# A weighted sum of two expert outputs: three buffers of 16 tokens for four of 12, a small first tile in a block of its own, and a double last-but-one store

## The chip, the cores and the metric

The kernel runs on one core of a Trainium2 chip. The core has a vector engine (VectorE, in the profile DVE), a scalar engine (ScalarE, ACT), and SyncE (SP), which here only issues DMAs. Transfers between the large memory (HBM) and the on-chip memory (SBUF, 128 partitions) are carried out by 16 DMA engines; SP and ACT each have a queue of their own that feeds all 16. The metric is the device time of one execution in microseconds; less is better.

## The reference

```python
"expert_outputs": np.random.randn(batch, seq, k, hidden)   # 16 x 1024 x 2 x 512, float32
"combine_weights": np.random.randn(batch, seq, k)          # 16 x 1024 x 2

weights = combine_weights[..., np.newaxis]
return np.sum(expert_outputs * weights, axis=2).astype(np.float32)
```

There are 16 x 1024 = 16,384 tokens. Each has two rows of 512 values (4 KB together), each row is multiplied by its own weight, and the two are added to one output row of 2 KB. 67.1 MB of rows are read and 33.6 MB are written.

## The kernel before

The tokens are spread over the 128 partitions, 128 tokens on each. In HBM they form two blocks: in the first, 120 neighbouring tokens belong to each partition (so the partitions' rows lie 120 x 4 KB = 480 KB apart in the input and 240 KB apart in the output); in the second, the last 8 per partition (32 KB and 16 KB apart). The function `rows` makes both views, and picks the block by the token's number.

Work goes in ten tiles of `J = 12` tokens per partition and a last one of `LAST = 8`. Each tile `et` is one of four buffers of 48 KB per partition (`bufs=4`). For each tile:

- SP loads it (line 75). One partition's part is contiguous in HBM, so it is one packet of 48 KB. The first tile is loaded in two pieces of 2 and 10 tokens, and the first of these is cut into packets of 4 KB by `max_dma_last_dim`.
- Tiles 0 to 8: VectorE multiplies all rows by their weights (line 84) and adds the two halves (line 85). Tile 9: ScalarE scales the first rows (line 92), VectorE the second ones (line 107) and adds (line 108). Tile 10, the last: ScalarE scales a token's first row (line 92), and VectorE does the second row's product and the sum in one instruction (line 96).
- The result `ot` overwrites the lower half of the tile's own buffer, and is stored from there: by ACT's queue in tiles 0 to 8 (line 86), by SP's in the last two (line 109).

A load into a buffer waits until the store of the tile that had it four tiles earlier has landed. The order on each engine is set by the framework's scheduler, which also inserts all waits. Before the first tile, ACT's queue writes 16 rows of zeros into the output (`ahead`, line 58; the results overwrite them later) and then loads the weights in two pieces, 120 and 8 KB (line 62).

Of the kernel before, what the change touches and what calls it, by code (L numbers as in the profile page):

```python
# [1 line left out]

# [4 lines left out]


@with_exitstack
def kernel(  # L10
    ctx: ExitStack,
    tc: tile.TileContext,
    expert_outputs: bass.AP,
    combine_weights: bass.AP,
    out: bass.AP,
):

    nc = tc.nc  # L20
    b, s, k, h = expert_outputs.shape
    assert k == 2
    n = b * s
    P = nc.NUM_PARTITIONS
    per = n // P
    assert per * P == n
    J, LAST = 12, 8
    main = per - LAST
    assert main % J == 0
    eo = expert_outputs.rearrange("b s k h -> (b s) (k h)")  # L30
    cw = combine_weights.rearrange("b s k -> (b s) k")
    o = out.rearrange("b s h -> (b s) h")

    def rows(x):

        a = x[0 : P * main, :].rearrange("(p t) f -> p t f", p=P)
        b = x[P * main : n, :].rearrange("(p t) f -> p t f", p=P)
        return lambda t, c: a[:, t : t + c, :] if t < main else b[:, t - main : t - main + c, :]

    eo, cw, o = rows(eo), rows(cw), rows(o)  # L40

    dt = mybir.dt.float32
    mult = mybir.AluOpType.mult
    add = mybir.AluOpType.add
    copy = mybir.ActivationFunctionType.Copy

    last = main // J

    wpool = ctx.enter_context(tc.tile_pool(name="w", bufs=1))
    ipool = ctx.enter_context(tc.tile_pool(name="in", bufs=4))  # L50

    wt = wpool.tile([P, per * k], dt)


    zt = wpool.tile([16, 128], dt)
    nc.vector.memset(zt, 0.0)  # L56
    first = out.rearrange("b s h -> (b s) h")[0 : P * main, :].rearrange("(q t) h -> q (t h)", q=16)
    ahead = nc.scalar.dma_start(out=first[:, 0:128], in_=zt)  # L58

    with tc.issue_after(ahead.ins):  # L60
        for t, c in ((0, main), (main, LAST)):
            nc.scalar.dma_start(
                out=wt[:, k * t : k * (t + c)].rearrange("p (t k) -> p t k", k=k), in_=cw(t, c)
            )
        warm = wpool.tile([P, 1], dt)
        nc.scalar.activation(out=warm, in_=nc.const_aps.tensor(1.0, (P, 1), dt), func=copy)  # L66

    for g in range(last + 1):
        et = ipool.tile([P, J, k * h], dt)

        ot = et.rearrange("p j f -> p (j f)")[:, 0 : J * h].rearrange("p (j f) -> p j f", f=h)
        t0, c = g * J, J if g < last else LAST

        for a, m in ((0, 2), (2, c - 2)) if g == 0 else ((0, c),):
            nc.sync.dma_start(  # L75
                out=et[:, a : a + m],
                in_=eo(t0 + a, m),
                max_dma_last_dim=k * h * 4 if g + a == 0 else None,
            )
        if g < last - 1:  # L80

            wb = wt[:, g * J * k : (g + 1) * J * k].unsqueeze(2).to_broadcast([P, J * k, h])
            ek = et.rearrange("p j (k h) -> p (j k) h", k=k)
            nc.vector.tensor_tensor(out=ek, in0=ek, in1=wb, op=mult)  # L84
            nc.vector.tensor_tensor(out=ot, in0=et[:, :, 0:h], in1=et[:, :, h : 2 * h], op=add)  # L85
            nc.scalar.dma_start(out=o(t0, c), in_=ot)
            continue


        for i in range(c):  # L90
            t = t0 + i
            nc.scalar.activation(  # L92
                out=et[:, i, 0:h], in_=et[:, i, 0:h], func=copy, scale=wt[:, 2 * t : 2 * t + 1]
            )
            if g == last:
                nc.vector.scalar_tensor_tensor(  # L96
                    out=ot[:, i, :],
                    in0=et[:, i, h : 2 * h],
                    scalar=wt[:, 2 * t + 1 : 2 * t + 2],
                    in1=et[:, i, 0:h],  # L100
                    op0=mult,
                    op1=add,
                )
        if g < last:
            w1 = wt.rearrange("p (t k) -> p t k", k=k)[:, t0 : t0 + c, 1:2]
            x1 = et[:, :, h : 2 * h]
            nc.vector.tensor_tensor(out=x1, in0=x1, in1=w1.to_broadcast([P, c, h]), op=mult)  # L107
            nc.vector.tensor_tensor(out=ot, in0=et[:, :, 0:h], in1=x1, op=add)  # L108
        nc.sync.dma_start(out=o(t0, c), in_=ot[:, 0:c])


# [1 line left out]
_INS = ['expert_outputs', 'combine_weights']  # L113
_OUTS = [((16, 1024, 512), 'float32')]


# [23 lines left out]
```

## Time and profile before

| | |
|---|---|
| Median of 3 runs | 239.11 us (239.08 to 239.12) |
| Span of the profiled execution, first to last instruction | 237.3 us |
| What lies around the span, against the median | 1.8 us |
| DVE busy | 194.1 us (82%) |
| ACT busy | 14.0 us (6%) |
| HBM read, written | 67.24 MB, 33.56 MB |
| DMAs of `et` loads | 2, then 10 tokens; nine of 12 tokens (6144 KB); one of 8 |
| Median time from issue to landing, loads of 12 tokens | 29.9 us |
| Median time from issue to landing, stores on ACT's queue | 33.0 us |

The profile is of one execution. Its span leaves out a little time at both ends, so times are compared through the medians of the runs, and places through the span. Queue q1 is SP's and q10 is ACT's. The share of a DMA queue is the time that its packets took, as a part of what 16 engines have in the span; a packet is one contiguous row that one engine moves, or the four bytes with which an engine signals its end. The granted TensorE clock is 1.000 and plays no part, as there are no matmuls. Times from issue to landing overlap each other: a DMA that was queued early waits long.

### The profile page before, as it was taken

What the parts mean: (1) busy time and instruction counts of PE and PEld (TensorE: products, weight loads), DVE (VectorE), ACT (ScalarE), POOL (GpSimd) and SP (SyncE); (2) the same over time, 40 slices, a digit from 0 to 9 for tenths busy, and PEclk for the clock granted to TensorE, in tenths of its full rate; (3) what the DMA queues carried; (4) which work ended last, traced back from release to release, by engine and by line L of the source; (5) the groups of instructions that cost most, each with busy time, mean ns of one, the idle gap of its engine ahead of it and who ended that gap; (6) DMA issues with size and microseconds to landing.
All of it is one profiled execution on the core that took longest, in us unless ns stands there. A gap on an engine that the chain in (4) does not pass through costs nothing.

```text
span 237.3 us, 157 instructions
## 1 busy us (share of the span) xinstructions
DVE 194.1 (82%) x29; ACT 14.0 (6%) x22; POOL 0.2 (0%) x4
## 2 busy tenths in 40 slices
DVE  0008999999999999999999889969996998785710
ACT  2000000000000000000000000000000000740800
POOL 0000000000000000000000000000000000000000
DMA  7999999989899999999898999999998979999997
GB/s 289 452 474 398 398 448 480 398 356 505 352 443 435 427 464 464 398 398 530 348 514 348 447 418 443 464 464 398 398 522 348 522 344 451 464 398 442 406 434 309
DMA packets 3760, 100.80 MB, mean 425 GB/s; under 512 B 544, under 2 KB 688, under 8 KB 944
## 3 DMA queue, kind: packets, MB, share of 16 engines
q1 hardware_dynamic: 2144, 72.35, 71.0%
q10 hardware_dynamic: 1616, 28.45, 27.9%
HBM read 67.24 MB, written 33.56 MB: 425 GB/s over the span
## 4 chain that ended last, share of the span: by engine, by line
DMA 59%; DVE 34%; ACT 2%; ACTq 0%; DVEq 0%; issue 0%; SPq 0%
DMA out_dram<-et 29%; DMA et<-in_expert_outputs_dram 23%; DVE et L84 22%; DVE et L85 11%; DMA wt<-in_combine_weights_dram 7%; ACT et L92 2%; DVE et L96 1%; DVEq L135 0%; ACTq L135 0%; ACTq L58 0%; DVE zt L56 0%; DVEq L84 0%; SPq L75 0%; ACTq L92 0%
## 5 line engine op out<-in xcount | busy, mean ns | idle before, releaser
L84 DVE TENSOR_TENSOR et<-et,wt 128x12288 f32<-128x12288 f32 x9 | 116.6, 12955 | 24.1 <-DMA wt<-in_combine_weights_dram 17.5
L85 DVE TENSOR_TENSOR et<-et 128x6144 f32<-128x6144 f32 x9 | 59.0, 6557 | 0.3
L92 ACT ACTIVATE et<-et,wt 128x512 f32<-128x512 f32 x20 | 12.5, 708 | 208.6 <-DMA et<-in_expert_outputs_dram 208.6
L96 DVE SCALAR_TENSOR_TENSOR et<-et,wt 128x512 f32<-128x512 f32 x8 | 5.6, 746 | 3.9 <-ACT et L92 3.6
L107 DVE TENSOR_TENSOR et<-et,wt 128x6144 f32<-128x6144 f32 x1 | 6.6, 6557 | 2.3 <-DMA et<-in_expert_outputs_dram 2.3
L108 DVE TENSOR_TENSOR et<-et 128x6144 f32<-128x6144 f32 x1 | 6.6, 6558 | 0.9 <-ACT et L92 0.9
L66 ACT ACT_TABLE_LOAD x1 | 1.3, 1283 | 2.4 <-issue 2.4
L56 DVE MEMSET zt<- 16x128 f32 x1 | 0.2, 165 | 0.8 <-PEq L124 0.8
L66 ACT ACTIVATE warm<-const-float32-1.0 128x1 f32<-128x1 f32 x1 | 0.2, 202 | 0.0
L124 POOL MEMSET const-bfloat16-1.0<- 128x1 bf16 x1 | 0.1, 102 | 0.0
L124 POOL MEMSET const-uint8-127<- 128x1 uint8 x1 | 0.1, 101 | 0.0
L124 POOL MEMSET const-float32-0.0<- 128x1 f32 x1 | 0.1, 99 | 0.2 <-issue 0.2
L124 POOL MEMSET const-float32-1.0<- 128x1 f32 x1 | 0.1, 98 | 0.0
## 6 DMA issues: line engine op xcount, KB each, us to landing
et<-in_expert_outputs_dram SPq DMA_DIRECT2D x9, 6144.0 KB, 29.9
out_dram<-et ACTq DMA_DIRECT2D x9, 3072.0 KB, 33.0
et<-in_expert_outputs_dram SPq DMA_DIRECT2D x1, 5120.0 KB, 17.0
et<-in_expert_outputs_dram SPq DMA_DIRECT2D x1, 4096.0 KB, 25.1
out_dram<-et SPq DMA_DIRECT2D x1, 3072.0 KB, 14.6
out_dram<-et SPq DMA_DIRECT2D x1, 2048.0 KB, 10.0
et<-in_expert_outputs_dram SPq DMA_DIRECT2D x1, 1024.0 KB, 5.0
wt<-in_combine_weights_dram ACTq DMA_DIRECT2D x1, 120.0 KB, 17.0
```

The costliest lines, as they stand in the source:

```text
L56: nc.vector.memset(zt, 0.0)
L66: nc.scalar.activation(out=warm, in_=nc.const_aps.tensor(1.0, (P, 1), dt), func=copy)
L84: nc.vector.tensor_tensor(out=ek, in0=ek, in1=wb, op=mult)
L85: nc.vector.tensor_tensor(out=ot, in0=et[:, :, 0:h], in1=et[:, :, h : 2 * h], op=add)
L92: nc.scalar.activation(out=et[:, i, 0:h], in_=et[:, i, 0:h], func=copy, scale=wt[:, 2 * t : 2 * t + 1])
L96: nc.vector.scalar_tensor_tensor(out=ot[:, i, :], in0=et[:, i, h : 2 * h], scalar=wt[:, 2 * t + 1 : 2 * t + 2], in1=et[:, i, 0:h], op0=mul ...
L107: nc.vector.tensor_tensor(out=x1, in0=x1, in1=w1.to_broadcast([P, c, h]), op=mult)
L108: nc.vector.tensor_tensor(out=ot, in0=et[:, :, 0:h], in1=x1, op=add)
L124: nc = _bacc.Bacc("TRN2", target_bir_lowering=False, num_devices=1)
```

## The change

- The tile sizes become 4, 12 and seven times 16 tokens. The first tile of 4 is a block of its own in HBM (its partitions' rows lie 16 KB apart in the input), and the other 124 tokens per partition are a second block (496 KB apart in the input, 248 KB in the output).
- One allocation `et` holds three rooms of 16 tokens each; tile g uses room g modulo 3. The load of tile g + 3 follows the store of tile g.
- Every tile is computed as the last one was: ScalarE scales the first row of a token, VectorE does the second product and the sum. Line by line these are the operations of lines 92 and 96 before.
- The seventh tile (number 6) is computed from its last token down, and its result lies in the upper half of its room; the eighth tile's result lies in the lower half of the next room. The two adjoin, and one DMA stores both, 32 tokens or 64 KB per partition.
- The last two stores go through SP's queue, the others through ACT's. The weights of the first tile (4 KB) are loaded by ACT's queue, the rest (124 KB) by SP's, right behind the load of the first tile. The first load isn't cut into packets of 4 KB any more.
- `tc.manual_schedule()` makes every engine issue in the order written. The waits are still inserted by the framework.

```diff
-    J, LAST = 12, 8
-    main = per - LAST
+    ROOM, ROOMS = 16, 3
+    TILES = [4, 12, 16, 16, 16, 16, 16, 16, 16]
+    STORES = [[0], [1], [2], [3], [4], [5], [6, 7], [8]]
+    main = TILES[0]
+    starts = [sum(TILES[:g]) for g in range(len(TILES))]
...
-    wpool = ctx.enter_context(tc.tile_pool(name="w", bufs=1))
-    ipool = ctx.enter_context(tc.tile_pool(name="in", bufs=4))
+    pool = ctx.enter_context(tc.tile_pool(name="all", bufs=1))
+    et = pool.tile([P, ROOMS * ROOM, k * h], dt)
+    halves = et.rearrange("p j (k h) -> p (j k) h", k=k)
...
+    def load(g):
+        at, c = g % ROOMS * ROOM, TILES[g]
+        nc.sync.dma_start(out=et[:, at : at + c], in_=eo(starts[g], c))
+
+    def weights(q, t, c):
+        q.dma_start(out=wt[:, k * t : k * (t + c)].rearrange("p (t k) -> p t k", k=k), in_=cw(t, c))
+
+    def combine(g, up):
+        at, c = g % ROOMS * ROOM, TILES[g]
+        base = k * at + (ROOM if up else 0)
+        for i in range(c - 1, -1, -1) if up else range(c):
+            t = k * (starts[g] + i)
+            x0, x1 = halves[:, k * (at + i), :], halves[:, k * (at + i) + 1, :]
+            nc.scalar.activation(out=x0, in_=x0, func=copy, scale=wt[:, t : t + 1])
+            nc.vector.scalar_tensor_tensor(
+                out=halves[:, base + i, :], in0=x1, scalar=wt[:, t + 1 : t + 2], in1=x0, op0=mult, op1=add
+            )
+        return base
...
+    with tc.manual_schedule():
+        nc.vector.memset(zt, 0.0)
+        ahead = flat[0 : P * main, :].rearrange("(q t) h -> q (t h)", q=16)
+        nc.scalar.dma_start(out=ahead[:, 0:128], in_=zt)
+        weights(nc.scalar, 0, main)
+        nc.scalar.activation(out=warm, in_=nc.const_aps.tensor(1.0, (P, 1), dt), func=copy)
+        load(0)
+        weights(nc.sync, main, per - main)
+        for g in range(1, ROOMS):
+            load(g)
+        for j, st in enumerate(STORES):
+            bases = [combine(g, up=len(st) == 2 and g == st[0]) for g in st]
+            c = sum(TILES[g] for g in st)
+            q = nc.sync if j >= len(STORES) - 2 else nc.scalar
+            q.dma_start(out=o(starts[st[0]], c), in_=halves[:, bases[0] : bases[0] + c, :])
+            for g in st:
+                if g + ROOMS < len(TILES):
+                    load(g + ROOMS)
```

The old loop over tiles, with its loads, its three ways to compute and its stores (lines 68 to 109), is removed.

More of the change, by code (lines that the diff above doesn't have):

```diff
@@ L26 @@
     assert per * P == n
-    J, LAST = 12, 8
-    main = per - LAST
[L29 to L32, printed above, removed]
-    def rows(x):
[L36 to L40, printed above, removed]
+    ROOM, ROOMS = 16, 3
+    TILES = [4, 12, 16, 16, 16, 16, 16, 16, 16]
+    STORES = [[0], [1], [2], [3], [4], [5], [6, 7], [8]]
+    assert sum(TILES) == per and [g for st in STORES for g in st] == list(range(len(TILES)))
+    main = TILES[0]
+    starts = [sum(TILES[:g]) for g in range(len(TILES))]
+    def rows(x):
+        first = x[0 : P * main, :].rearrange("(p t) f -> p t f", p=P)
+        second = x[P * main : n, :].rearrange("(p t) f -> p t f", p=P)
+        return lambda t, c: first[:, t : t + c, :] if t < main else second[:, t - main : t - main + c, :]
+    flat = out.rearrange("b s h -> (b s) h")
+    eo = rows(expert_outputs.rearrange("b s k h -> (b s) (k h)"))
+    cw = rows(combine_weights.rearrange("b s k -> (b s) k"))
+    o = rows(flat)
     dt = mybir.dt.float32
@@ L45 @@
     copy = mybir.ActivationFunctionType.Copy
-    last = main // J
-    wpool = ctx.enter_context(tc.tile_pool(name="w", bufs=1))
-    ipool = ctx.enter_context(tc.tile_pool(name="in", bufs=4))
[L52 to L63, printed above, removed]
-            )
-        warm = wpool.tile([P, 1], dt)
-        nc.scalar.activation(out=warm, in_=nc.const_aps.tensor(1.0, (P, 1), dt), func=copy)
@@ L68 @@
[L68 to L109, printed above, removed]
@@ new lines @@
+    pool = ctx.enter_context(tc.tile_pool(name="all", bufs=1))
+    et = pool.tile([P, ROOMS * ROOM, k * h], dt)
+    halves = et.rearrange("p j (k h) -> p (j k) h", k=k)
+    wt = pool.tile([P, per * k], dt)
+    zt = pool.tile([16, 128], dt)
+    warm = pool.tile([P, 1], dt)
+    def load(g):
[3 more added lines that the diff above has]
+        q.dma_start(out=wt[:, k * t : k * (t + c)].rearrange("p (t k) -> p t k", k=k), in_=cw(t, c))
@@ new lines @@
+    with tc.manual_schedule():
[3 more added lines that the diff above has]
+        weights(nc.scalar, 0, main)
+        nc.scalar.activation(out=warm, in_=nc.const_aps.tensor(1.0, (P, 1), dt), func=copy)
+        load(0)
[5 more added lines that the diff above has]
+            c = sum(TILES[g] for g in st)
+            assert bases[-1] == bases[0] + sum(TILES[g] for g in st[:-1])
+            q = nc.sync if j >= len(STORES) - 2 else nc.scalar
[3 more added lines that the diff above has]
+                    load(g + ROOMS)
```

## The prediction

> **What bounds the kernel now.** I read the page first, its summary of engines, its 40 slices and its DMA section.
>
> ```profile
> DVE 194.1 (82%) x29; ACT 14.0 (6%) x22; POOL 0.2 (0%) x4
> ...
> DMA  7999999989899999999898999999998979999997
> ...
> DMA packets 3760, 100.80 MB, mean 425 GB/s; under 512 B 544, under 2 KB 688, under 8 KB 944
> ## 3 DMA queue, kind: packets, MB, share of 16 engines
> q1 hardware_dynamic: 2144, 72.35, 71.0%
> q10 hardware_dynamic: 1616, 28.45, 27.9%
> ```
>
> VectorE is busy 82% of the span, but the two queues together hold the 16 DMA engines for 71.0 + 27.9 = 98.9% of it. The traffic sets the time, not the arithmetic. The next question is where the missing 1.1% lies, so I cut the span into windows (columns: microseconds, busy time of each engine, granted clock, DMA share, GB/s).
>
> ```profile
> 0.00:1.75 1.75, 0.17 (x1) 0.00 (x0) 0.20 (x4) 1.00 0.00 0
> 1.75:2.75 1.00, 0.00 (x0) 0.37 (x1) 0.00 (x0) 1.00 0.90 143
> ...
> 38.00:41.00 3.00, 3.00 (x2) 0.00 (x0) 0.00 (x0) 1.00 0.84 344
> 41.00:48.00 7.00, 7.00 (x1) 0.00 (x0) 0.00 (x0) 1.00 1.02 414
> 48.00:200.00 152.00, 145.11 (x16) 0.00 (x0) 0.00 (x0) 1.00 1.01 435
> ...
> 236.20:237.30 1.10, 0.00 (x0) 0.00 (x0) 0.00 (x0) 1.00 0.00 0
> ```
>
> Nothing moves in the first 1.75 us and the last 1.1 us; between them the engines never stand still, and from 48 to 200 us they hold 435 GB/s. (A large packet counts where it starts, so short windows jump.) Last, who waits, and how the last tile's arithmetic runs, from the waits of the SP queue and the timeline:
>
> ```profile
> SPq L75 <- DMA out_dram<-et: 174.1, 7, 45.8
> ```
>
> ```profile
> 38.04 141.23 ACTq L86 DMA_DIRECT2D out_dram<-et  x8
> ...
> 219.90 5.01 ACT L92 ACTIVATE et<-et,wt 128x512 f32<-128x512 f32 x8 [9.48 <-DMA et<-in_expert_outputs_dram]
> 220.66 5.78 DVE L96 SCALAR_TENSOR_TENSOR et<-et,wt 128x512 f32<-128x512 f32 x8 [3.65 <-ACT et L92]
> ```
>
> The loads wait for stores to free their buffers, yet the load queue always holds an earlier load meanwhile. ScalarE and VectorE overlap: eight tokens take 226.44 - 219.90 = 6.54 us together.
>
> **The packet account.** The trace's packet records give the price of size. One packet is one contiguous row of one partition: 16 KB 611 ns, 24 KB 912, 32 KB 1213, 40 KB 1514, 48 KB 1815. Each further 8 KB costs 301 ns, that is 27.2 GB/s per engine. The records of one engine overlap by 3 to 4 ns, so a packet costs some 4.6 ns beyond its bytes; a semaphore packet of 4 bytes (one per engine and DMA, 9 ns) shifts the next by some 6 ns. Per engine before:
> - bytes: 100.80 MB / 16 / 27.2 GB/s = 231.63 us
> - 3760 packets less 26 DMAs x 16 semaphores = 3344, 209 per engine, x 4.6 ns = 0.96
> - 26 semaphores x 6.2 ns = 0.16
> - start: the 16 packets of 4 KB take 194 ns in the mean where 159 is usual, 0.57; the engines' first packets start 0.14 after the first one in the mean
> - 44 load packets around the first store (40.9 to 47 us) take up to 2.33 us instead of 1.82: 0.61 per engine
>
> Sum 234.07. With the first packet at 1.79, the mean engine ends at 235.9, which the records show (235.7 to 236.14). The rest of the span of 237.3 follows the last packet: landing, semaphores, the closing drain. The median of 239.11 lies 1.8 us over the span, and I keep that.
>
> **The change, part by part.**
> - Bytes: the same. The first zero write and the weights (120 + 8 KB become 4 + 124 KB) sum to the same bytes.
> - Packets: a load of 4, 12 or 16 tokens is 128 rows of 16, 48 or 64 KB; nine loads give 1152. Eight stores give 1024, weights 256, zero write 16: 2448, or 153 per engine. 56 fewer x 4.6 ns = -0.26 us. By the line above, a 64 KB packet takes 2.417 us and the store of 32 tokens is 64 KB too.
> - DMAs: 9 + 8 + 2 + 1 = 20 instead of 26; six semaphores x 6.2 ns = -0.04. The Trainium skill (DMA: Bandwidth & Descriptors, Anatomy of one DMA) puts a fixed cost of about 2.0 us on each DMA of the GpSimd path; charged end to end, six fewer would bring 12 us. No row here shows such a charge between queued DMAs: the next packet begins 3 ns after a semaphore's.
> - The start: eight packets of 16 KB replace sixteen of 4 KB on each engine. Only the first one or two of an engine were slow (195 to 1071 ns, then 159). Bounds: the 0.57 us vanishes, or comes again when the second tile first touches the block with the wide pitch. I take it as unchanged, for the slow packets come first whatever their row.
> - The first store: bounds 0 and twice 0.61 (store of tile 0, then of tile 1, in another block). I take it unchanged, by the row of before's own second block: the 32 KB load packets took 1213 ns and its 16 KB store packets 611, without any excess.
> - Pitch: before, partitions lie 480 KB apart (stores 240), after it 496 (248). At 480, only those 44 of 1152 load packets were far off 1815 ns, by 0.61 x 16 / 44 = 0.22 us or 12%. Bounds: nothing, and 12% on all loads of the wide block (124 tokens, 149 us), 18 us. I take nothing, the row of the other 1108.
> - The Trainium skill (same page, Latency and other measured facts) warns of row pitches at large powers of two and gives 207 GB/s at 512 KB against 214 padded. If 496 KB behaved so, 3.4% of the wide block's 224 us of traffic, 7.6 us, would be added (an estimate from that page). No run here shows 512 KB.
> - Arithmetic: VectorE's two passes (19.5 us per 12 tokens) and their 194 us give way to 128 scalings at 708 ns on ACT and 128 fused steps at 0.72 us pace on DVE, some 91 and 92 us. It all lies beside DMA. The weights no longer land after 17 us, and that too is worth nothing: in those 17 us the engines were moving loads.
> - Rooms: three of 16 tokens instead of four of 12, the same 192 KB per partition. This can only cost, by leaving the load ring empty. A tile takes 0.78 + 16 x 0.72 = 12.3 us. Load g+3 can be issued once store g lands: some 12.3 + 8 x (2.42 + 1.21) = 29.0, plus 1.5 for issue and landing, 43 us after load g landed. Meanwhile the ring holds loads g+1 and g+2, 2 x 19.35 us, and store g itself takes 9.7 us of the engines: 48.4 of work for 43 us. The cover is 5.5 us at least. At the start: store 0 is issued near 11 us, its first packet follows some 5.3 us later (43.3 after 38.04 before), eight packets beside 48 KB ones need 17: landed near 34, while loads 0 to 2 keep the ring busy beyond 43.
> - The end, on SP: behind the wait for store 5, SP holds load 8, behind it the two last stores. The double store comes 12.3 + 1.5 us after load 7 landed; load 8 runs 19.35 us meanwhile, cover 5.5. The last store comes as long after load 8; the double store runs 19.34 us, cover 5.5. Each us beyond a cover costs one us.
> - ACT's queue: a store waits for DVE's last step, behind it stand the scalings of the next tile. Some 1 us per tile, within those covers. The small weights on SP stand behind load 0: eight packets of 45 ns, already counted in the bytes.
>
> Sum: -0.26 - 0.04 = -0.30; span 237.0, time 239.11 - 0.30 = **238.8 us**. A measurement of this kernel tells 0.2%, 0.48 us, from no change, so this counts as the same.
>
> **Rivals.**
> - The cold spots shrink (faster, 0.28). Contiguous first rows and a small first store may remove most of 0.57 + 0.61: 238.8 - 1.2 = 237.6 at best, 238.2 with half. For it: the excess lies exactly at the first load and the first store. Against: it may belong to being first, not to the rows. It counts as faster from a further 0.18 us on.
> - Cold spots come twice (slower, 0.08): the wide block pays anew in loads and stores, +1.2, 240.0. Against: before's second block paid nothing.
> - ACT and DVE take turns instead of overlapping (slower, 0.07). Place: the last three tiles. One token then takes 0.708 + 0.746 = 1.45 us, a tile 23.3: 11 us later than reckoned, which exceeds the three covers of 5.5 by 5.5 each, 16.5 us: 255. It decides from a pace of 0.72 + 5.5/16 = 1.06 us per token. Against: the timeline shows 5.78 us for eight.
> - The pitch slows packets (slower, 0.05): +18, 257 at the worst; it decides from (0.30 + 0.48) / 149 = 0.5% on each load packet. Against: 1108 packets at a like pitch.
> - 64 KB rows are cut in two, so the change does not do what it says (0.05): 64 more packets per engine x 4.6 ns = +0.29, 239.1, the same.
> - The forecast keeps 0.47.
>
> Same 0.52, faster 0.28, slower 0.20. The range reaches down to half of the cold spots gone, 238.2 less 0.1 for a bit more, and up to 239.7, some three quarters of the cold spots paid anew; the dear slow cases stay outside.
>
> **What would show it.** After: 2448 + 20 x 16 = 2768 packets, 1728 on q1 and 1040 on q10; 3792 if 64 KB is cut. DMA share 0.00 only in the first 1.8 and last 1.2 us; DVE and ACT busy near 90 us each; load packets of 64 KB at 2.417 us. A DMA window below 0.9 around the loads of the eighth and ninth tile, or near the end, means a cover was too short. Load packets above 2.42 us all along mean the pitch. A span off by over 0.5 us with full windows would mean that the start or the first stores changed.

## The result, and the profile after

The changed kernel takes 240.57 us in the median of seven runs (240.47 to 241.04), the kernel before 239.12 beside it: a ratio of 1.0061, interval 1.0047 to 1.0074. It is slower by 1.45 us, where 0.3 us less was forecast. The profiled execution took 240.50 us with a span of 238.7, 1.36 us more than before's 237.3.

The page of after, the same parts as shown of before:

```profile
span 238.7 us, 415 instructions
...
DVE 87.3 (37%) x129; ACT 80.9 (34%) x130; POOL 0.2 (0%) x4
...
DMA  7997999899999999989899999989898989898994
...
DMA packets 2771, 100.83 MB, mean 422 GB/s; under 512 B 448, under 2 KB 592, under 8 KB 592
## 3 DMA queue, kind: packets, MB, share of 16 engines
q1 hardware_dynamic: 1728, 79.82, 77.9%
q10 hardware_dynamic: 1040, 20.98, 20.4%
q14 instruction: 3, 0.02, 0.0%
```

The packets are as counted, 2768 on two queues. But there is a third queue, q14, of kind instruction, with three packets that before's page did not have. I take them for the program's own code, fetched while it runs (below, a fetch): their number follows the number of instructions in the runs below. The instructions went from 157 to 415. In the windows (microseconds, busy time of each engine, clock, DMA share, GB/s) the engines still never stand still together, and hold the same rate:

```profile
0.00:1.75 1.75, 0.17 (x1) 0.00 (x0) 0.20 (x4) 1.00 0.06 19
...
60.00:200.00 140.00, 55.10 (x82) 49.55 (x80) 0.00 (x0) 1.00 1.00 435
200.00:237.00 37.00, 11.69 (x18) 9.91 (x16) 0.00 (x0) 1.00 0.94 408
237.00:238.70 1.70, 0.00 (x0) 0.00 (x0) 0.00 (x0) 1.00 0.00 0
```

The forecast covers held. From the timeline:

```profile
1.62 180.50 SPq L62 DMA_DIRECT2D et<-in_expert_outputs_dram  x8
...
189.00 9.91 ACT L73 ACTIVATE et<-et,wt 128x512 f32<-128x512 f32 x16 [15.34 <-DMA et<-in_expert_outputs_dram]
189.75 11.07 DVE L74 SCALAR_TENSOR_TENSOR et<-et,wt 128x512 f32<-128x512 f32 x16 [14.17 <-ACT et L73]
200.85 19.70 SPq L96 DMA_DIRECT2D out_dram<-et  x2
208.35 9.91 ACT L73 ACTIVATE et<-et,wt 128x512 f32<-128x512 f32 x16 [9.44 <-DMA et<-in_expert_outputs_dram]
```

ACT and VectorE overlap: 16 tokens take 200.82 - 189.00 = 11.8 us (12.3 reckoned). The double store was issued at 200.85, while load 8 ran until 208.3: 7.5 us of cover.

**Where the time went** shows only when the sixteen DMA engines are taken apart. The records don't name the engine, but each packet begins 3 or 4 ns before the one ahead of it on the same engine ends, so they can be chained engine by engine. The excess of a packet is its time less the usual time of its size; a gap is time between two data packets of a chain. This account, in us, is worked out from the records of the two profiled executions:

| | before, mean of 16 engines | after, mean | after, slowest engine |
|---|---|---|---|
| excess in the first 10 us | 0.57 | 0.99 | 0.96 |
| excess from 10 to 33 us | 0.02 | 0.07 | 0.00 |
| excess from 33 to 50 us (first large store) | 0.58 | 0.54 | 0.38 |
| excess later | 0.01 | 0.13 | 0.99 |
| gaps in the chain | 0.06 | 0.06 | 0.60 |
| last packet ends at | 235.94 | 236.15 | 237.29 |

Before's slowest engine ended at 236.14, 0.21 behind the mean; after's ended 1.14 behind it. So the 1.36 us of span are: the mean engine +0.21, the slowest engine's lag +0.93, and the time from the last packet to the span's end +0.21 (1.20 before, 1.41 after; I have not traced that last part). The slowest engine of after is the one that carried two of the three instruction packets: each of 8 KB and 309 ns leaves a gap of 302 ns, and the 64 KB packet behind it takes 530 or 457 ns longer than 2418. That is 0.60 + 0.99 = 1.59 us; in its other rows that engine was 0.26 better than the mean, and the mean itself has 0.19 in these two, so 1.14 is left. The windows show the late engine too, first before, then after:

```profile
235.00:236.00 1.00, 0.00 (x0) 0.00 (x0) 0.00 (x0) 1.00 0.62 262
236.00:237.00 1.00, 0.00 (x0) 0.00 (x0) 0.00 (x0) 1.00 0.00 0
```

```profile
235.00:236.00 1.00, 0.00 (x0) 0.00 (x0) 0.00 (x0) 1.00 0.38 164
236.00:237.00 1.00, 0.00 (x0) 0.00 (x0) 0.00 (x0) 1.00 0.08 33
```

### The profile page after: what moved, and what is told of

It reads as the page before. It is cut to its first block, busy times and chain, and to the rows that moved or that the text cites. A ratio compares the mean times of both kernels' runs of the same rounds, so it can differ in the third digit from the quotient of the medians.

```text
span 238.7 us, 415 instructions
## 1 busy us (share of the span) xinstructions
DVE 87.3 (37%) x129; ACT 80.9 (34%) x130; POOL 0.2 (0%) x4
## 3 DMA queue, kind: packets, MB, share of 16 engines
q1 hardware_dynamic: 1728, 79.82, 77.9%
q10 hardware_dynamic: 1040, 20.98, 20.4%
## 4 chain that ended last, share of the span: by engine, by line
DMA 80%; DVE 7%; ACT 4%; issue 1%; ACTq 0%; DVEq 0%; SPq 0%
DMA et<-in_expert_outputs_dram 39%; DMA out_dram<-et 38%; DVE et L74 7%; ACT et L73 4%; DMA wt<-in_combine_weights_dram 3%; DVEq L125 0%; ACTq L125 0%; ACTq L83 0%; DVE zt L80 0%; SPq L62 0%; DVEq L74 0%; ACTq L73 0%
## 5 line engine op out<-in xcount | busy, mean ns | idle before, releaser
L74 DVE SCALAR_TENSOR_TENSOR et<-et,wt 128x512 f32<-128x512 f32 x128 | 87.2, 745 | 132.0 <-ACT et L73 130.2
L73 ACT ACTIVATE et<-et,wt 128x512 f32<-128x512 f32 x128 | 79.4, 707 | 135.4 <-DMA et<-in_expert_outputs_dram 130.0
```

The lines of the kernel that those rows point to most:

```text
L73: nc.scalar.activation(out=x0, in_=x0, func=copy, scale=wt[:, t : t + 1])
L74: nc.vector.scalar_tensor_tensor(out=halves[:, base + i, :], in0=x1, scalar=wt[:, t + 1 : t + 2], in1=x0, op0=mult, op1=add)
```

## The experiments

Times are medians, ratios are against the kernel before on the same chip. A lag, below, is how far the slowest engine is behind the middle one when both signal the end of a load or store on q1 (0.19 us in before from 50 us on, 1.34 at the end of after).

**Which part is it: first block, first packets, double store?** Three runs on after, each one edit.

after_4k:
```diff
-        nc.sync.dma_start(out=et[:, at : at + c], in_=eo(starts[g], c))
+        ... max_dma_last_dim=k * h * 4 if g == 0 else None
```


> After, with the first load cut into rows of 4 KB as before; all else unchanged. If the excess at the start (0.985 us per engine against 0.565 before) comes from the 16 KB packets, it falls back to some 0.57 and the time by 0.4 to 240.2. If it comes from the first tile's narrow block, it stays, and the time stays at 240.6.

Measured 240.78 us, ratio 1.0069 (1.0051 to 1.0087). The excess in the first 10 us stayed at 0.90. The packet size of the first load is not what makes the start slower.

after_wide:
```diff
-    main = TILES[0]
+    main = per - TILES[-1]                       # the weights then come in three pieces
```


> After, with the blocks moved: the first 112 tokens of a partition are one block (448 KB apart), so the first tile of 4 is read with the wide pitch, and the last tile of 16 is a block of its own; the weights come in three pieces. If the narrow first block makes the start slower, the excess at the start falls to some 0.57 us and the time by 0.4 to 240.2. If the packet size does, the time stays at 240.6; if the wide pitch of 496 KB costs something later, it falls too, but with the start unchanged.

Measured 240.66 us, ratio 1.0059 (1.0042 to 1.0077). The excess at the start fell to 0.69, most of the way to the 0.57 expected of the first block, but the excess from 33 to 50 us rose from 0.54 to 1.06. What was won was lost 30 us later, and the time stayed.

after_single:
```diff
-    STORES = [[0], [1], [2], [3], [4], [5], [6, 7], [8]]
+    STORES = [[0], [1], [2], [3], [4], [5], [6], [7], [8]]
```


> After with the seventh and eighth tile stored one by one (on SP's queue) instead of as one row of 64 KB; instructions nearly the same. Theory of the instruction fetches: 240.6, as after, the same three fetches. Rival (the double store or its packets make the end late): faster by 0.5 or more, 240.1 or below.

Measured 240.59 us, ratio 1.0062 (1.0050 to 1.0074), as after. The double store shows no price and no gain here.

**The first block in before.** before_narrow:
```diff
-        a = x[0 : P * main, :]
+        a = x[0 : P * J, :]        # and so for the second block and the weights
```


> The kernel before with its blocks moved: the first tile of 12 tokens is a block of its own (48 KB apart), the other 116 tokens are the second block (464 KB apart); instructions and tiles unchanged. If the narrow first block costs 0.3 to 0.4 us at the start, as in after against after_wide (0.985 against 0.685 us of excess), the excess there rises from 0.57 to some 0.9 and the time to 239.5. If that excess is made up later (around 35 to 45 us, where after_wide lost what it had won), or comes from the small first tile, the time stays at 239.1.

Measured 240.06 us (239.53 to 240.76), ratio 1.0039 (1.0024 to 1.0055). Slower, but not at the start: the excess there was 0.48, so a narrow first block of 12 tokens costs nothing there. It was 0.89 instead of 0.58 from 33 to 50 us, and seven of the engines took the first store packet one place earlier in their order than the rest. Neither of the two expectations had this.

**Instruction fetches in before.** The two clean ones add ACT instructions that nobody waits for (the order on ACT and VectorE is fixed as written here):
```diff
             nc.scalar.dma_start(out=o(t0, c), in_=ot)
+            for _ in range(40 if g < 8 else 0):      # 12 in the other
+                nc.scalar.activation(out=warm, in_=nc.const_aps.tensor(1.0, (P, 1), dt), func=copy)
```


> The kernel before with 40 one-element ACT instructions behind each of the first eight stores (320 more; some 9 us per tile in which ACT would idle), VectorE and all DMAs unchanged. ACT then holds some 370 instructions. Theory of the instruction fetches: three fetches of 8 KB on q14, all for ACT and on one DMA engine, which falls behind the other fifteen by 3 x 0.25 to 0.55 us; the time rises by 0.7 to 1.6 us to 239.8 to 240.7. Rival (instruction count plays no part): 239.1.

> The same with 12 instead of 40 (96 more, ACT some 150 as in after): one fetch. Theory of the instruction fetches: one engine falls behind by 0.25 to 0.55 us, and as the slowest engine of before is 0.19 us behind the middle one already, the time rises by 0.1 to 0.5, to 239.2 to 239.6. Rival: 239.1.

With 40: 240.81 us, ratio 1.0068 (1.0055 to 1.0081). With 12: 239.34 us, ratio 1.0013 (1.0005 to 1.0022). The pages show that nothing else changed; first the one with 40, then the one with 12:

```profile
q1 hardware_dynamic: 2144, 72.35, 70.6%
q10 hardware_dynamic: 1616, 28.45, 27.7%
q14 instruction: 3, 0.02, 0.0%
```

```profile
q1 hardware_dynamic: 2144, 72.35, 71.0%
q10 hardware_dynamic: 1616, 28.45, 27.9%
q14 instruction: 1, 0.01, 0.0%
```

Everything but q14 is before's, to the packet. In the one with 40 the middle engine ends at 236.03 us, against 235.95 in before; one engine's lag climbs from 0.27 to 0.47, 1.11 and 1.76 us behind the three fetches (61.7, 122.1 and 185.4 us). The time follows that one engine: +1.67 us for a lag of +1.57. The windows show it as a single engine's share after the rest have ended (1/16 is 0.06; a packet counts where it starts):

```profile
235.00:236.00 1.00, 0.00 (x0) 0.00 (x0) 0.00 (x0) 1.00 0.69 295
236.00:237.00 1.00, 0.00 (x0) 0.00 (x0) 0.00 (x0) 1.00 0.04 16
237.00:238.00 1.00, 0.00 (x0) 0.00 (x0) 0.00 (x0) 1.00 0.04 16
```

Two more runs on before were to show the same, and a second effect came on top. before_many:
```diff
+    def tiny(acts, dves):   # one-element instructions
             nc.scalar.dma_start(out=o(t0, c), in_=ot)
+            tiny(12, 18)
```


> The kernel before with 108 one-element ACT instructions and 162 one-element VectorE fills added behind the tiles, so that its engines hold about as many instructions as after; DMAs, tiles and rows unchanged. Theory of the instruction fetches: three more 8 KB packets of kind instruction appear on q14 in mid run, each holds up one DMA engine by 0.3 to 0.5 us, and the time rises by 0.4 to 1.2 us (239.5 to 240.3). Rival (the packets of 64 KB, the first block or the double store are the cause, the instruction count plays no part): 239.1, the same as before.

before_tok (all tiles computed as the last one):
```diff
-        if g < last - 1:        # the two large VectorE instructions, and those of tile 9
...
+        (nc.scalar if g < last - 1 else nc.sync).dma_start(out=o(t0, c), in_=ot[:, 0:c])
```


> The kernel before with only the arithmetic of the change: all tiles are computed token by token (ACT scales the first row, VectorE does product and sum), so that ACT and VectorE hold some 150 and 200 instructions; blocks, tiles of 12, four buffers, packets and stores as before. Theory of the instruction fetches: two fetches for VectorE on one DMA engine and one for ACT on another; the slowest engine ends 0.8 to 1.2 us behind the middle one instead of 0.19, and the time is 239.7 to 240.2. Rival (layout, packets and rooms are the cause): 239.1.

before_many took 244.73 us, ratio 1.0227 (1.0208 to 1.0246): the 18 fills cost VectorE 2.2 us per tile, it fell behind, and the DMA engines ran dry for 5.5 us near the end. before_tok took 242.45, ratio 1.0139 (1.0123 to 1.0154): with the last tiles of 12 and 8 and this faster arithmetic, the stores are gone before the last tile is computed, and the engines ran dry for 3.2 us:

```profile
226.00:230.00 4.00, 2.05 (x3) 3.02 (x5) 0.00 (x0) 1.00 0.94 406
230.00:235.00 5.00, 3.51 (x6) 1.99 (x4) 0.00 (x0) 1.00 0.34 144
235.00:240.60 5.60, 0.00 (x0) 0.00 (x0) 0.00 (x0) 1.00 0.77 325
```

Each had three fetches. In before_many the lag stood at 1.65 us behind two of them, and behind the third one engine ran into the gap 2.5 us after the middle one; in before_tok it stood at 1.85 us behind two and 2.69 behind the third. The gap then wiped it out (0.09 and 0.08 at the end): all engines went on from it together. So the times say nothing on the fetches. The lags are more than the fetches themselves make up: an engine that a fetch had delayed lost another 0.8 us (before_many, on seven packets) and 1.0 us (before_tok, on four) within the next 35 us, which the engines of before_act40 did not.

**Instruction fetches in after.** after_act40 adds 40 of the same ACT instructions behind each of the first six stores:
```diff
+            for _ in range(40 if j < 6 else 0):
+                nc.scalar.activation(out=warm, in_=nc.const_aps.tensor(1.0, (P, 1), dt), func=copy)
```


> After with 40 one-element ACT instructions behind each of the first six stores (240 more, in time that ACT would idle). ACT's fetches rise from one to two or three, all on its own DMA engine, which was 0.2 us late by its one fetch. Theory of the instruction fetches: that engine falls 0.8 to 1.9 us behind the middle one and, where it exceeds VectorE's engine, sets the end: 240.5 to 241.2. Rival: 240.6.

Measured 241.43 us, ratio 1.0094 (1.0079 to 1.0109), five fetches, lag 2.23 at the end: another 0.86 us over after, a little over the range. The other direction failed twice. after_few and after_lean:
```diff
+    BIG = (2, 3, 4, 5, 7)       # (2,) in after_lean
+        if g in BIG:            # ACT's scalings, then one product and one sum of 16 tokens on VectorE
```


> After, with VectorE's 16 fused steps in tiles 2 to 5 and 7 replaced by two large ones each (a product and a sum of 16 tokens, as lines 107 and 108 of before), so that VectorE has some 110 instructions instead of 208; ACT and all DMAs unchanged. Theory of the instruction fetches: VectorE's two fetches shrink to one or none, and the slowest DMA engine ends 0.5 to 1.0 us earlier: 239.6 to 240.1. Rival (first block, packets or double store): 240.6, as after.

> After with tile 2 alone computed by ACT's scalings and two large VectorE instructions, so that VectorE has some 183 instructions instead of 208 and its second fetch (at 217 us, when 200 of its instructions had run) should not come. The tile takes some 6 us longer, within the 9 us by which its successor's load was early. Theory of the instruction fetches: two fetches instead of three, time lower by 0.2 to 0.5 us, 240.1 to 240.4. Rival: 240.6, as after.

after_few: 242.99 us, ratio 1.0153 (1.0127 to 1.0179); after_lean: 242.81, ratio 1.0146 (1.0129 to 1.0163). The fetches fell to two in each, as meant (a third packet on after_few's page has 32 bytes and comes at 0.17 us), yet the time rose by over 2 us. In after_few the tile before the double store took 18.6 us, the cover ended, and the engines were idle for 1.4 us at 208 to 210. In both, all sixteen engines lost some 1.15 us on packets from 105 to 108 us, at a place where after loses 0.03. I can't say what these are; the stores and loads stand differently from tile 2 on.

**The fetches out, the DMAs as they were.** after_plain computes one product per tile and leaves out the second scaling and the sum, so that few instructions are left:
```diff
-        for i in range(c - 1, -1, -1) if up else range(c):
-            nc.scalar.activation(...)
-            nc.vector.scalar_tensor_tensor(...)
+        n = {4: 7, 8: 12, 12: 17, 16: 23}[c]
+        nc.vector.tensor_tensor(out=x, in0=x, in1=wb, op=mult)      # x: n rows of the tile
```


> After with each tile's 32 scalings and fused steps (24 and 8 in the small tiles) replaced by one VectorE product of about the same duration (12.4 us for 16 tokens); it leaves out the second scaling and the sum, so its output is not the weighted sum. All DMAs, rows and queues are those of after, and no engine has more than some 40 instructions. Theory of the instruction fetches: no fetch in the span, the slowest engine ends 0.3 to 0.8 us behind the middle one instead of 1.34, and the time falls by 0.5 to 1.0 us to 239.6 to 240.1. Rival (layout alone): 240.6, as after.

Measured 241.11 us (240.47 to 241.33), ratio 1.0065 (1.0043 to 1.0086). There was no fetch, and the mean engine ended at 235.78, 0.37 us earlier than after's. But the time did not fall, against the 239.6 to 240.1 expected: one engine, late from the start, was 1.88 us behind at the end. So the fetches alone do not explain after. The packet records show what that engine did; the first line is one of the fifteen others (L is a load packet, s a store packet, with its size in KB, start in us and time in ns):

```text
L64@34.87+2418 L64@37.28+2418 s24@39.70+912 L64@40.60+2520
L64@35.35+2427 s24@37.77+912 L64@38.68+3420
```

The second store is issued at about 34.1 us. Fifteen engines take its first packet after two more load packets. This one began its load packet later, at 35.35 instead of 34.5 to 34.9, and took the store right after it. My reading is that each engine chooses its next packet ahead, and that the store came in between these choices; the records show the order only. From then on the engine is out of step with the others, and its next load packet takes 3.42 us instead of 2.4 to 2.8; at 65 us it loses another 0.45. In after itself four engines did the same (their packets at 38.3 to 38.6 us took 3.16 to 3.25 us) and ended at 236.28 to 236.97.

after_plain_wide and after_plain_480 change the blocks without fetches:
```diff
-    main = TILES[0]
+    main = per - TILES[-1]                       # after_plain_wide
-    TILES = [4, 12, 16, ...]
+    TILES = [8, 8, 16, ...]                      # after_plain_480
```


> The kernel without fetches (one product per tile, sum left out) with the blocks of after_wide: first tile read with a wide pitch of 448 KB, last tile a block of its own. If the narrow first block costs what is left over before, the excess at the start falls by 0.3 us and the time below after_plain by 0.2 to 0.5. If not, the same as after_plain.

> The kernel without fetches (one product per tile, sum left out) with tiles of 8, 8 and seven times 16 and the first block of 8, so that the rest has the pitch of before, 480 KB. If the pitch of 496 KB costs something (through the slow packets at 35 to 45 us or later), below after_plain by 0.2 us or more; otherwise the same within 0.2.

240.21 us, ratio 1.0043 (1.0025 to 1.0061), and 239.58, ratio 1.0011 (0.9988 to 1.0033), with runs from 239.17 upward. Both are below after_plain, by 0.9 and 1.5 us, more than expected. In the first, the start's excess fell from 0.79 to 0.62, and three engines lagged by 1.1 to 1.2 us at the end, again from the 35 us store on. The profile of the second is of a run of 243.00 us and doesn't stand for its median, and it differs in three things at once (pitch, first block, size of the first two tiles). So this is no proof against the pitch of 496 KB: the usual 64 KB packet took 2418 ns at it, as the line of sizes gives. It does show that without fetches the layout moves the time by 0.9 to 1.5 us, nearly as much as three fetches did in before_act40 (1.67); which part of the layout, and whether it acts only through the lag, is not shown.

**Out of the edge.** Last, the second store was issued some 1 us later, so that no engine stands at the edge (the moment that divides engines that take the store after one load packet from those that take it after two).

after_plain_delay:
```diff
-        n = {4: 7, 8: 12, 12: 17, 16: 23}[c]
+        n = {4: 7, 8: 12, 12: 19, 16: 23}[c]
```


> after_plain (no fetches; one product per tile, second scaling and sum left out) with the product of the second tile two rows longer, so that the second store is issued some 1.1 us later, at about 35.2 us. Theory that engines fall out of step at that store: all sixteen engines take its first packet in the same slot, the slowest engine ends 0.2 to 0.5 us behind the middle one instead of 1.9, and the time falls to 239.0 to 239.6. Rival (the late engine is late whatever the slot): 240.5 to 241.1, as after_plain.

after_delay:
```diff
+            for _ in range(12 if j == 1 else 0):
+                nc.scalar.activation(out=warm, in_=nc.const_aps.tensor(1.0, (P, 1), dt), func=copy)
```


> After with 12 one-element ACT instructions ahead of the second store, which is so issued some 1 us later (about 35.0 us); fetches as in after. Theory of both (fetches and step): the engines keep step at that store, but VectorE's two fetches still hold one engine 1.1 to 1.6 us behind: 240.2 to 240.6. If only the step counts: 239.0 to 239.6.

In both profiled executions all sixteen engines took the store in the same place (39.6 to 40.4 us). after_plain_delay: the mean engine ended at 235.70, the slowest at 236.51, and that execution took 239.70 us. Its twelve runs fall in two groups, 239.15 to 239.76 and 240.47 to 241.22, the median of 240.12 (ratio 1.0042, 1.0025 to 1.0059) between them and in neither expected range; what the second group has is not known, as none of it was profiled. after_delay, with fetches: 240.89 us, ratio 1.0075 (1.0062 to 1.0088), no better than after and above the expected range. Fifteen engines ended by 236.15, and one at 237.30. It carried two fetches (gaps of 0.30 us each, later excess 1.11 us). In the windows it stands alone:

```profile
235.00:236.00 1.00, 0.00 (x0) 0.00 (x0) 0.00 (x0) 1.00 0.01 0
236.00:237.00 1.00, 0.00 (x0) 0.00 (x0) 0.00 (x0) 1.00 0.08 33
237.00:238.00 1.00, 0.00 (x0) 0.00 (x0) 0.00 (x0) 1.00 0.00 0
```

| | fetches as in after | no fetches |
|---|---|---|
| second store at the edge | 240.57 (after) | 241.11 (after_plain) |
| second store later | 240.89 (after_delay) | 240.12, half of the runs at 239.15 to 239.76 (after_plain_delay) |

The two causes do not add up where they hit different engines; the later engine decides. In after that was the engine with two fetches (237.29, against 236.97 for the last one out of step), in after_plain the one out of step (237.50), in after_delay again one with two fetches (237.30). Taking one cause away left the other in charge. This rests on one profiled execution of each, and what a lost step costs differs between them.

## Why the prediction was wrong, step by step

- **Packets, DMAs and sizes** (-0.30): right. The counts came out at 2768, 1728 and 1040, the 64 KB packet at 2418 ns. With neither fetches nor a broken step (after_plain_delay) the mean engine ended at 235.70 against 235.94, 0.24 us earlier; its excess was then as large in sum as before's (0.32 more at the start, 0.31 less at the first large store).
- **The start** ("I take it as unchanged"): wrong, and near the upper bound. The excess was 0.99 instead of 0.57 us, +0.42, which alone eats the saving. The packet size is not the reason (0.90 when cut to 4 KB). The excess was 0.78 to 0.99 in all nine profiled executions with the first block of 4 tokens, and 0.62 and 0.69 with the tile read at a wide pitch. But the block of 12 in before_narrow had 0.48, so what about the small block costs this time is not shown.
- **The first store** ("unchanged"): right for the mean (0.54 against 0.58), wrong for the engines, of which four lost 0.74 to 0.92, the other twelve 0.36 to 0.63, and the four fell out of step. (In before single engines lost up to 0.83 here as well, yet all ended within 0.24 us of the mean.)
- **Arithmetic** ("It all lies beside DMA"): this is the step that failed most. The time of the arithmetic does lie beside the transfers, but its instructions do not: they are fetched by the same sixteen DMA engines. I priced the 256 new operations by the time of the engine that runs them, and not by the bytes of their code. In their place the runs showed three fetches of 8 KB; the engine with two of them lost 1.59 us to them and ended 1.14 us behind the mean.
- **The sum itself**: it was made for the mean engine. The other engines did not help a late one out (in before_act40 one worked on alone for 1.5 us after the rest had ended), so the end is the slowest one's. Of the 1.36 us, 0.93 are lag. Before had 0.21 of it, and I wrote its range (235.7 to 236.14) down as a check, not as a term. My sign of being wrong, a span off by over 0.5 us with full windows, came true (238.7 for 237.0), but pointed to the start and the first stores alone.
- **Rooms and end**: right. The engines did not run dry; the runs that shortened a cover (before_tok, after_few) show the price, 3.2 and 1.4 us.
- **Rivals**: ACT and VectorE did not take turns, 64 KB rows were not cut, the pitch shows no price on the usual packet. Of the two on cold spots (the slow packets at the start and the first store), the one that had them shrink was wrong, and the one that had them come twice was right in part, at the start only. No rival had the fetches or the lag.

The Trainium skill (Runtime: NRT & Kernel Launch, Instruction fetch mechanics) says that a sequencer fetches its next page through a DMA queue of its own and that the cost of crossing a 16 KiB boundary is "mostly hidden". The runs agree on the queue and differ on the size and the cost: packets of 8 KB, and 0.55 to 0.85 us on one DMA engine each, which stays hidden while that engine has time to spare: ACT's fetch in after cost nothing, as its engine ended at 236.41, 0.88 us ahead of the slowest.

Left open: the two groups of after_plain_delay; the 0.21 us after the last packet; what makes the start slower; which part of the layout made after_plain_wide and after_plain_480 faster than after_plain; why a large store's first packets hold up all engines until 39.7 us, and why an engine out of step loses more; the 1.15 us at 105 us in after_few and after_lean.

## What to carry to other kernels

When transfers fill all DMA engines from end to end, look at the slowest engine, not at the mean share: the end of the kernel is the last engine's, and work put on one engine alone counts in full. Count the instructions that a change adds: in after, VectorE's first fetch came behind 79 recorded ones and its second 121 later, and on a kernel without idle DMA time a fetch is paid where its engine is the last one. When a cause is taken away and the time stays, look for a second one that was hidden behind the first before calling the first one innocent.

## What the runs showed of the hardware

- Instruction fetches ran as 8 KB packets on q14. VectorE's came after 79 and 200 of its recorded instructions in after, at 87.1 and 217.2 us, on the same DMA engine; ACT's at 93.3 us on another. One fetch left a gap of 0.30 us and made the data packet behind it 0.24 to 0.54 us longer (after, before_act40, before_many).
- A packet costs 4.6 ns beyond its bytes, from 4 KB to 64 KB; the line of sizes held to within 1 ns at 64 KB (2417 reckoned, 2418 measured).
- Engines in step took the first 24 KB store packet within 0.7 us of each other, with up to 0.5 us lost on the load packet ahead of it; one out of step lost 0.7 to 1.0 us on one load packet.
